# Up-projections of a ConvFFN: the weights' sums and the mixing products on VectorE in place of GpSimd, with VectorE's steps of a tile in a new order

## The chip, the cores and the metric

One core of a Trainium2 chip runs the whole network in one launch. The metric is the time of one execution on the device in microseconds (us). Engines are named as in the profile: PE (TensorE, matmuls), PEld (its weight loads), DVE (VectorE), ACT (ScalarE), POOL (GpSimd), SP (SyncE, which issues all the DMAs spoken of here).

## The reference, cut to what matters

Two layers over 1024 latent tokens and 256 context tokens of width 1024. Each layer ends with a ConvFFN, and the change touches only its up-projection:

```python
D_FF = 2816
def conv_ffn(h, w_up, conv_w, conv_b, w_down):
    a = h @ w_up                                   # 1024 x 5632
    g, u = a[..., :D_FF], a[..., D_FF:]
    gp = jnp.pad(g, ((0, 0), (1, 1), (0, 0)))      # along the tokens
    acc = conv_b + gp[:, 0:T]*conv_w[0] + gp[:, 1:T+1]*conv_w[1] + gp[:, 2:T+2]*conv_w[2]
    return (jax.nn.silu(acc) * u) @ w_down
...
# modulation columns of all layers: silu(c) @ w_mod + b_mod
```

In layer 0 latents and context both go through it, in layer 1 the latents alone. All of it is float32.

## The kernel before

The 2816 features are worked off in 22 tiles of 128 features (`f` = 0 to 21); `head` does the first two and sets up, `turn(f)` does one tile, `end` closes. Features lie on partitions, tokens along the row. Tokens come in chunks: 0 and 1 are the two halves of the latents (512 each), 2 is the context (256).

**Seven products in place of eight.** For the latents, gate and up-projection of a tile are one 2x2 block product: rows are gate weights (`a1`, loaded as `raw[f, 0]`) and up weights (`a2`, `raw[f, 1]`), each cut into two halves of 512 input features (`a11`, `a12`, `a21`, `a22`); columns are the two token halves. Sums of the operands save one of the eight products: s1 = a21 + a22, s2 = s1 - a11, s3 = a11 - a21, s4 = a12 - s2 for the weights (`sum`, line 1694; done on POOL for every tile), and t1 to t4 for the tokens, made once in `head`. The seven products are numbered as in `PROD`; in a turn PE does 6, 5, 7 of tile f, then 1 of the next tile n = f + 1, (context, gate weights, of n), 3 of f, 2 of n, (context, up weights, of f), 4 of f. Products 6, 7 and 4 add up in one bank `y`, 5 and 3 in `z`, 1 and 2 in `x`; ACT and DVE read a bank between two of its products, and the next product may start only then.

**Each product is three matmuls for each quarter of its input,** since every operand is a high part (`...h`, rounded by a cast) and a low part (`...l`, the rest): 12 matmuls of 128x512. The high parts of the s are cast by ACT (`high`, L1698), those of a1 by POOL (`ahigh`, L1678) and of a2 by ACT (L1676); all low parts are subtractions on DVE (`low`, L1702; `alow`, L1683).

**After the products,** with g and su rows of a tile: `s1` (L1984, ACT) copies product 1 out of bank x before product 2 adds to it; `u2` (L1988, DVE) reads bank y after product 6 and before 7; `u3` (L1997) and `c22` (L2000) read y and z after 7; `c12` (L2003) reads z after 3; `c21` (L2006) reads y after 4, in the next turn. `c11` (L1994, ACT) copies bank x after product 2. Then the convolution along the tokens: `conv` (L2013, ACT: centre tap), `conv2` (L2017 and L2018, DVE: the two neighbours), `silu` (L2021, ACT), and `mix` (L2024: times u). The mix of chunks 0 and 1 is done on POOL in the next turn, that of the context on DVE. `store` (L2042) sends su to DRAM, for the down-projection.

**Beside it, in layer 0,** `mod` (L321, DVE; L326, POOL, adds 1 to some columns) works off 53 modulation columns of 1024 products each, for one or both of the two condition vectors, up to three columns in a turn. Each needs its weights in `wm`, a tile with one buffer.

**Order.** PE, DVE, ACT and POOL run their instructions in the order in which the code is written. SP's order is not fixed by hand here; a scheduler places the DMAs. `raw` has two buffers, so `raw[n, 0]` can be loaded when s4 of f has been summed, and `raw[n, 1]` when `alow(f, 1)` is done.

Of the kernel before, what the change touches and what calls it, by code (L numbers as in the profile page):

```python
# [44 lines left out]
def backbone(tc, a):  # L45
    nc = tc.nc
    V, S, P, PE, dma = nc.vector, nc.scalar, nc.gpsimd, nc.tensor, nc.sync
# [1020 lines left out]
    po[3].out(2)  # L1068
    po[2].parts(1)
    turn()  # L1070
    evac(1, 1, b1_1)
    w1 = window(1)
# [547 lines left out]
    class Up:  # L1620
# [144 lines left out]
        def head(self, w, b00, n1):  # L1765
# [49 lines left out]
            x = {k: xlp.tile([128, NLAT], F32, name=f"x{k}", tag=f"x{k}") for k in (2, 3)}  # L1815
            self.spare["st"] = [x[2][:, :512], x[2][:, 512:], x[3][:, :512]]
            for n in ("s1", "s2", "s3"):
                self.sum(2, n)
            self.fs[2] = F(self, 2)
            self.product(2, 1)  # L1820
            self.high(2, "s2")
# [21 lines left out]
            for j, p in enumerate(parts[2:]):  # L1843
                p.high(4, xs(j + 4))
                p.low(4)
            self.sum(2, "s4")
            self.high(2, "s4")
            self.low(2, "s4")
            x.update({k: xlp.tile([128, NLAT], F32, name=f"x{k}", tag=f"x{k}") for k in (6, 7)})
# [5 lines left out]
        def turn(self, f):  # L1855

            me, old = self.fs[f], self.fs[f - 1]
            n = f + 1 if f < NF - 1 else None
            ctx = 2 in self.chunks
            self.product(f, 6)  # L1860
            if f > 2:
                old.c21()
            if n:
                self.load(n, 0)
                self.ahigh(n, 0, P)
            else:
                down = self.down = Down(self)
                down.load(0)
                for e in (0, 1):
                    down.act_load(e)  # L1870
            if f > 2:
                old.mix(1)
                old.mix(0)
                old.store()
            self.ahigh(f, 1, S)
            self.product(f, 5)
            if not n:
                down.act_split(0)
            if f > 3:
                me.u2()  # L1880
            else:
                me.s1()
                me.u2()
                me.c11(True)
            if n:
                self.alow(n, 0)
            self.alow(f, 1)
            if n:
                self.load(n, 1)
            else:  # L1890
                down.load(1)
            if f > 2:
                self.mod()
            self.product(f, 7)
            if not n:
                down.act_split(1)
                self.context(f, 1)
            if n:
                for s in ("s1", "s2", "s3"):
                    self.sum(n, s)  # L1900
                new = self.fs[n] = F(self, n)
                self.product(n, 1)
            me.u3()
            me.c22()
            if f == 2:
                old.rest()
            else:
                self.mod()
            if not n:
                down.split(0)  # L1910
            else:
                if n > 3:
                    new.s1()
                new.open()
                self.context(n, 0)
                new.gate(2)
                for s in ("s2", "s1", "s3"):
                    self.high(n, s)
                    self.low(n, s)
            self.product(f, 3)  # L1920
            me.c12()
            for c in (0, 1):
                me.conv(c)
                me.conv2(c)
            self.mod()
            if n:
                self.product(n, 2, "w" if n == 3 else None)
                if n > 3:
                    new.c11()
                self.sum(n, "s4")  # L1930
                self.context(f, 1)
            for c in self.chunks:
                if c == 2:
                    me.conv(2)
                    me.conv2(2)
                me.silu(c)
            if n:
                self.high(n, "s4")
                self.low(n, "s4")
            if ctx:  # L1940
                me.mix(2, V, self.bank[f, "c", 1])
            self.product(f, 4)

        def end(self):

            me = self.fs[NF - 1]
            self.down.split(1)
            me.c21()
            me.mix(0, V)
            me.mix(1)  # L1950
            me.store()

    class F:
# [323 lines left out]
    down = up.down  # L2277
# [19 lines left out]
    for d in range(8):  # L2297
        f = down.product(1, d, (NF - 4, NF - 3))
# [608 lines left out]
    down = up.down  # L2907
# [296 lines left out]
```

## Time and profile before

| | us |
|---|---|
| median of 3 runs | 2892.46 (2890.66 to 2894.56) |
| the profiled execution | 2893.4 |
| its span, first to last instruction | 2891.5 |
| up-projection of layer 0, tiles 2 to 21 (first matmul of tile 2 to first matmul of tile 21) | 765.11 to 1263.86 |
| up-projection of layer 1, the same | 2222.86 to 2605.07 |

The rows quoted further down give the start of an instruction in us from the span's start, its length, engine, source line, operation and tiles, and in brackets the idle time of the engine before it and what ended that. In the chain of waits each row is start, length, engine and line. Groups give the count, the busy time and the mean of one in ns. A busy PE is not a PE at its peak: matmuls overlap, so what a tile costs is read from the start of one tile to the start of the next.

### The profile page before, as it was taken

What the parts mean: (1) busy time and instruction counts of PE and PEld (TensorE: products, weight loads), DVE (VectorE), ACT (ScalarE), POOL (GpSimd) and SP (SyncE); (2) the same over time, 40 slices, a digit from 0 to 9 for tenths busy, and PEclk for the clock granted to TensorE, in tenths of its full rate; (3) what the DMA queues carried; (4) which work ended last, traced back from release to release, by engine and by line L of the source; (5) the groups of instructions that cost most, each with busy time, mean ns of one, the idle gap of its engine ahead of it and who ended that gap; (6) DMA issues with size and microseconds to landing.
All of it is one profiled execution on the core that took longest, in us unless ns stands there. A gap on an engine that the chain in (4) does not pass through costs nothing.

```text
span 2891.5 us, 40129 instructions
## 1 busy us (share of the span) xinstructions
PE 2782.2 (96%) x14654; PEld 2315.7 (80%) x14654; DVE 2246.1 (78%) x3648; ACT 1243.8 (43%) x2518; POOL 1072.6 (37%) x1066
## 2 busy tenths in 40 slices
PE   7988999999999999999999998999999999999997
PEld 3857888887888887888888777999877777777886
DVE  5688888879888887778777887888668666669766
ACT  5525888824433332331002445888634333333104
POOL 2142444762244445421012443444331445552112
PEclk9999999999999999999999999999999999999998
DMA  6144001283143433363221010000141222226311
GB/s 229 70 141 139 15 24 58 85 276 107 49 133 127 134 114 122 130 234 112 68 72 50 30 37 23 1 1 1 39 139 49 80 81 86 75 95 227 94 59 59
DMA packets 97229, 264.89 MB, mean 92 GB/s; under 512 B 11908, under 2 KB 21060, under 8 KB 96904
## 3 DMA queue, kind: packets, MB, share of 16 engines
q1 hardware_dynamic: 97032, 262.33, 27.1%
q8 instruction: 115, 1.88, 0.3%
q14 instruction: 82, 0.67, 0.1%
HBM read 212.53 MB, written 49.75 MB: 91 GB/s over the span
## 4 chain that ended last, share of the span: by engine, by line
PE 46%; DVE 16%; DMA 4%; issue 4%; POOL 3%; ACT 3%; DVEq 0%; POOLq 0%; SPq 0%; ACTq 0%
PE d L72 18%; PE y L72 4%; PE p L72 4%; PE b L72 4%; PE pv L1277 3%; DMA raw<-in_wup 3%; PE x L72 3%; PE z L72 2%; POOL x L1694 2%; PE T L1264 2%; DVE x L2017 2%; DVE x L2018 2%; DVE a2l L1683 1%; PE S L1197 1%; PE qk L72 1%
## 5 line engine op out<-in xcount | busy, mean ns | idle before, releaser
L2100 DVE SCALAR_TENSOR_TENSOR x<-d,mod,x 128x512 f32<-128x512 f32 (+1 forms) x352 | 255.0, 735 | 95.6 <-PE d L72 93.4
L1246 POOL TENSOR_SCALAR p<-p,sm 128x1280 f32<-128x1280 f32 x128 | 171.3, 1338 | 288.3 <-DVE sm L1245 199.7
L1267 DVE TENSOR_TENSOR tl<-T,th 128x512 fp32r<-128x512 f32 x328 | 225.5, 687 | 46.7 <-ACT th L1266 41.3
L1277 PE MATMUL pv<-th,v 128*128 128x256 f32 x976 | 254.1, 309 | 1.4 <-ACT vo L1406 1.0
L1220 DVE TENSOR_REDUCE mx<-S 128x1 f32<-128x512 f32 (+1 forms) x400 | 233.9, 585 | 11.0 <-PE S L1199 3.8
L72 PE MATMUL d<-act,wh 128*128 128x512 f32 (+1 forms) x832 | 232.0, 365 | 0.0
L1266 ACT CAST th<-T 128x512 fp32r<-128x512 f32 x328 | 192.2, 586 | 84.4 <-PE T L1264 76.5
L2083 ACT CAST act<-act 128x512 fp32r<-128x512 f32 (+1 forms) x110 | 61.5, 577 | 383.8 <-PE d L72 215.5
L1694 POOL TENSOR_TENSOR x<-raw 128x512 f32<-128x512 f32 x80 | 119.4, 1492 | 271.8 <-DMA raw<-in_wup 191.7
L72 PE MATMUL b<-h,wh 128*128 128x512 f32 (+1 forms) x752 | 207.8, 364 | 6.0 <-DVE h L489 4.1
L1264 PE MATMUL T<-ident,p 128*128 128x128 f32 x1280 | 193.0, 272 | 1.5 <-POOL p L1246 1.5
L72 PE MATMUL x<-h,a1h 128*128 128x512 f32 x608 | 190.9, 395 | 0.0
L1264 PEld LDWEIGHTS T<-ident,p 128*128 128x128 f32 x1280 | 156.5, 140 | 34.9 <-POOL p L1246 3.2
L1277 PE MATMUL pv<-tl,v 128*128 128x256 f32 x656 | 177.4, 282 | 0.0
L1277 PEld LDWEIGHTS pv<-th,v 128*128 128x128 f32 x976 | 173.4, 189 | 2.4 <-ACT vo L1406 1.5
L72 PEld LDWEIGHTS d<-act,wh 128*128 128x128 f32 x832 | 149.8, 189 | 27.2
L72 PEld LDWEIGHTS b<-h,wh 128*128 128x128 f32 x752 | 133.6, 190 | 36.4 <-DVE h L489 5.5
L2024 POOL TENSOR_TENSOR su<-x,su 128x512 f32<-128x512 f32 x78 | 131.3, 1696 | 55.4 <-DVE su L2006 44.3
L72 PE MATMUL d<-act,wl 128*128 128x512 f32 (+1 forms) x416 | 151.8, 365 | 0.0
L1984 ACT COPY su<-x 128x512 f32<-128x512 f32 x40 | 23.4, 586 | 289.6 <-PE x L72 209.1
L1237 ACT ACTIVATE p<-S,mx,rq 128x512 f32<-128x512 f32 (+1 forms) x192 | 136.2, 712 | 12.4 <-DVE mx L1228 10.8
L72 PE MATMUL b<-h,wl 128*128 128x512 f32 (+1 forms) x376 | 136.3, 363 | 2.5 <-DVE wl L111 2.4
(520 smaller groups left out, 8205.0 us busy)
## 6 DMA issues: line engine op xcount, KB each, us to landing
raw<-in_wup SPq DMA_DIRECT2D x86, 512.0 KB, 3.4
wm<-in_wmod SPq DMA_DIRECT2D x72, 512.0 KB, 3.6
act<-d_act SPq DMA_DIRECT2D x88, 256.0 KB, 4.0
raw<-in_wdn SPq DMA_DIRECT2D x44, 512.0 KB, 4.4
raw<-in_wout SPq DMA_DIRECT2D x32, 512.0 KB, 3.3
d_act<-su SPq DMA_DIRECT2D x22, 640.0 KB, 3.0
d_act<-su SPq DMA_DIRECT2D x22, 512.0 KB, 2.9
raw<-in_win SPq DMA_DIRECT2D x20, 512.0 KB, 3.6
```

The source lines that it names most:

```text
L72: PE.matmul(out, w, x, start=first and i == 0, stop=last and i == n - 1, skip_group_check=more)
L1220: V.reduce_max(mx[:, j : j + 1], s, axis=AX.X)
L1237: S.activation(o, s, AF.Exp, scale=self.scale, bias=self.mx[:, 3:4], accum_out=self.sm[:, j : j + 1])
L1246: P.tensor_scalar(out=self.p, in0=self.p, scalar1=sm[:, 3:4], scalar2=1.0, op0=ALU.mult, op1=ALU.mult)
L1264: PE.transpose(tb[:, (2 * j + i) * 128 : (2 * j + i) * 128 + 128], rows[i].p[:, c : c + 128], ident)
L1266: S.copy(hi, tb)
L1267: V.tensor_sub(lo, tb, f32(hi))
L1277: PE.matmul(out[0], st, mv, start=(u + j == 0 and x == 0), stop=(u + j == n - 1 and x == len(ops) - 1))
L1694: eng.tensor_tensor(out=t, in0=self.src(f, x), in1=self.src(f, y), op=op)
L2024: eng.tensor_mul(self.s_of(c), self.t[c], self.s_of(c) if u is None else u)
L2083: S.copy(hi, f32(lo))
L2100: V.scalar_tensor_tensor(out=x, in0=b, scalar=mod[self.l, c // 2][:, 40 + d : 41 + d], in1=x, op0=ALU.mult, op1=ALU.add)
```

## The change

All four sums of a tile and the mix of chunks 0 and 1 go from POOL to DVE. In a turn the sums s1 to s3 come after `c22`, and right behind them the casts and low parts of s2, s1, s3; the copy `s1` of product 1 comes after those casts. `conv(0)` is issued ahead of `c12`, `silu` right behind each `conv2`; s4's sum, cast and low part come ahead of the context's convolution, then the mix of chunk 1; the mix of chunk 0 comes in the next turn behind `c21`. In layer 0 the second `mod` of a turn stands behind the low parts and the third at the turn's end; turn 2 now has two where it had one. The arithmetic is the same.

```diff
@@ head
             for n in ("s1", "s2", "s3"):
-                self.sum(2, n)
+                self.sum(2, n, V)
...
-            self.sum(2, "s4")
+            self.sum(2, "s4", V)
@@ turn
             self.product(f, 6)
             if f > 2:
                 old.c21()
+                old.mix(0, V)
+                old.store()
             if n:
                 self.load(n, 0)
                 self.ahigh(n, 0, P)
...
-            if f > 2:
-                old.mix(1)
-                old.mix(0)
-                old.store()
...
             if n:
-                for s in ("s1", "s2", "s3"):
-                    self.sum(n, s)
                 new = self.fs[n] = F(self, n)
                 self.product(n, 1)
             me.u3()
             me.c22()
             if f == 2:
                 old.rest()
-            else:
-                self.mod()
-            if not n:
-                down.split(0)
-            else:
+            if n:
+                for s in ("s1", "s2", "s3"):
+                    self.sum(n, s, V)
+                for s in ("s2", "s1", "s3"):
+                    self.high(n, s)
+                    self.low(n, s)
                 if n > 3:
                     new.s1()
                 new.open()
                 self.context(n, 0)
                 new.gate(2)
-                for s in ("s2", "s1", "s3"):
-                    self.high(n, s)
-                    self.low(n, s)
+            else:
+                down.split(0)
+            self.mod()
             self.product(f, 3)
+            me.conv(0)
             me.c12()
+            me.conv(1)
             for c in (0, 1):
-                me.conv(c)
                 me.conv2(c)
-            self.mod()
+                me.silu(c)
             if n:
                 self.product(n, 2, "w" if n == 3 else None)
                 if n > 3:
                     new.c11()
-                self.sum(n, "s4")
-                self.context(f, 1)
-            for c in self.chunks:
-                if c == 2:
-                    me.conv(2)
-                    me.conv2(2)
-                me.silu(c)
-            if n:
+                self.sum(n, "s4", V)
                 self.high(n, "s4")
                 self.low(n, "s4")
+                self.context(f, 1)
+            me.mix(1, V)
             if ctx:
+                me.conv(2)
+                me.conv2(2)
+                me.silu(2)
                 me.mix(2, V, self.bank[f, "c", 1])
+            self.mod()
             self.product(f, 4)
@@ end
             me.mix(0, V)
-            me.mix(1)
```

Instructions as issued, at three places. The first is DVE in one tile of layer 1, from `alow(f, 1)` on, before (x2_22105 and so on are the spare tiles that hold sums and convolutions):

```order
L1683 TENSOR_TENSOR a2l_22028<-raw_22821,a2h_22027 128x512
L1997 TENSOR_TENSOR su_22838<-y_22921,su_22838 128x512
L2000 TENSOR_TENSOR su_22838<-z_22942,su_22838 128x512
L1702 TENSOR_TENSOR s2l_22996<-x2_22105,s2h_22995 128x512
L1702 TENSOR_TENSOR s1l_23000<-x2_22105,s1h_22999 128x512
L1702 TENSOR_TENSOR s3l_23004<-x3_22106,s3h_23003 128x512
L2003 TENSOR_TENSOR g_22855<-z_22942,x6_22224 128x512
L2017 SCALAR_TENSOR_TENSOR x6_22224<-g_22855,convw_61,x6_22224 128x512
L2018 SCALAR_TENSOR_TENSOR x6_22224<-g_22855,convw_61,x6_22224 128x512
```

The same stretch of DVE with the change (line numbers from 1860 on are up to 4 lower):

```order
L1683 TENSOR_TENSOR a2l_22028<-raw_22821,a2h_22027 128x512
L1993 TENSOR_TENSOR su_22835<-y_22922,su_22835 128x512
L1996 TENSOR_TENSOR su_22835<-z_22942,su_22835 128x512
L1694 TENSOR_TENSOR x2_22105<-raw_22958 128x512
L1694 TENSOR_TENSOR x2_22105<-x2_22105,raw_22938 128x512
L1694 TENSOR_TENSOR x3_22106<-raw_22938,raw_22958 128x512
L1702 TENSOR_TENSOR s2l_22992<-x2_22105,s2h_22991 128x512
L1702 TENSOR_TENSOR s1l_22996<-x2_22105,s1h_22995 128x512
L1702 TENSOR_TENSOR s3l_23000<-x3_22106,s3h_22999 128x512
L1999 TENSOR_TENSOR g_22867<-z_22942,x6_22224 128x512
L2013 SCALAR_TENSOR_TENSOR x6_22224<-g_22867,convw_61,x6_22224 128x512
```

Three sums now stand on DVE between c22 and the low parts. The second place is ACT in a tile of layer 1, before:

```order
L1676 CAST a2h<-raw 128x512
L1984 COPY su<-x 128x512
L1698 CAST s2h<-x_22106 128x512
L1698 CAST s1h<-x_22105 128x512
L1698 CAST s3h<-x_22105 128x512
L2013 ACTIVATE x_22225<-g,convw 128x512
```

and ACT with the change:

```order
L1676 CAST a2h<-raw 128x512
L1698 CAST s2h<-x_22106 128x512
L1698 CAST s1h<-x_22105 128x512
L1698 CAST s3h<-x_22105 128x512
L1980 COPY su<-x 128x512
L2009 ACTIVATE x_22225<-g,convw 128x512
```

The copy that frees bank x for product 2 moved behind the three casts. The third place is SP in a tile of layer 0 (raw: up-projection weights, wm: modulation weights, d_act: the store), before:

```order
L307 DMA wm_9316<-in_wmod 128x1024
L2042 DMA d_act0_7024<-su_9027 128x1280
L1644 DMA raw_9417<-in_wup 128x1024
L307 DMA wm_9421<-in_wmod 128x1024
L307 DMA wm_9455<-in_wmod 128x1024
L1644 DMA raw_9600<-in_wup 128x1024
```

and SP with the change:

```order
L307 DMA wm_9371<-in_wmod 128x1024
L2038 DMA d_act0_7024<-su_9027 128x1280
L1644 DMA raw_9421<-in_wup 128x1024
L307 DMA wm_9424<-in_wmod 128x1024
L307 DMA wm_9503<-in_wmod 128x1024
L1644 DMA raw_9606<-in_wup 128x1024
```

Nothing moved in SP's order: although the code now asks for the store ahead of the load of the next gate weights, that load (the last row) is still placed ahead of the next store.

## Rows read from the trace of the kernel before

**Rows 1.** The page: the span, and busy time (share of the span) and instructions of each engine.

```profile
span 2891.5 us, 40129 instructions
PE 2782.2 (96%) x14654; PEld 2315.7 (80%) x14654; DVE 2246.1 (78%) x3648; ACT 1243.8 (43%) x2518; POOL 1072.6 (37%) x1066
```

**Rows 2.** Timeline of PE: the first matmul of product 6, which opens a tile; tiles 3, 4, 5, 6 and 21 of layer 0, then tiles 2, 4, 9, 10 and 21 of layer 1.

```profile
790.37 0.39 PE L72 MATMUL y<-h,s2h 128*128 128x512 f32 x1
820.00 0.63 PE L72 MATMUL y<-h,s2h 128*128 128x512 f32 x2
845.25 0.39 PE L72 MATMUL y<-h,s2h 128*128 128x512 f32 x1
870.50 0.39 PE L72 MATMUL y<-h,s2h 128*128 128x512 f32 x1
...
1263.86 0.63 PE L72 MATMUL y<-h,s2h 128*128 128x512 f32 x2
...
2222.86 0.40 PE L72 MATMUL y<-h,s2h 128*128 128x512 f32 x1
2264.97 0.62 PE L72 MATMUL y<-h,s2h 128*128 128x512 f32 x2
2366.01 0.39 PE L72 MATMUL y<-h,s2h 128*128 128x512 f32 x1
2385.46 0.39 PE L72 MATMUL y<-h,s2h 128*128 128x512 f32 x1
2605.07 0.39 PE L72 MATMUL y<-h,s2h 128*128 128x512 f32 x1
```

**Rows 3.** Timeline of PE: the first matmul of product 7, with the idle time before it, in tile 3 of layer 0 and in tile 21 of layer 1.

```profile
798.93 1.22 PE L72 MATMUL y<-h,s3h 128*128 128x512 f32 x2 [2.84 <-DVE x L1988]
...
2614.34 1.19 PE L72 MATMUL y<-h,s3h 128*128 128x512 f32 x2 [3.56 <-DVE x L1988]
```

**Rows 4.** The chain of waits in layer 1, tiles 10 and 11 (start, length, what): once round, from one end of a2l to the next.

```profile
2392.45 1.72 DVE a2l L1683
2394.19 3.92 DMA raw<-in_wup
2398.24 1.30 POOL x L1694
...
2400.92 0.63 ACT s2h L1698
...
2408.49 0.61 ACT s4h L1698
...
2410.56 0.60 DVE x L1988
2411.15 1.13 DVE a1l L1683
2412.29 1.71 DVE a2l L1683
```

**Rows 5.** The chain of waits in layer 0, tiles 13 and 14.

```profile
1077.38 0.44 POOL mod L326
1077.82 1.27 POOL x L1694
1079.10 4.50 DMA raw<-in_wup
...
1107.69 4.07 DMA raw<-in_wup
```

**Rows 6.** Groups of DVE's and POOL's instructions in layer 1, tiles 4 to 20 (us 2264 to 2605; count | busy us, mean ns of one | idle before), and one line of who waited for whom in the same stretch (us in total, times, longest).

```profile
L2017 DVE SCALAR_TENSOR_TENSOR x<-g,convw,x 128x512 f32<-128x512 f32 x35 | 33.9, 970 | 0.0
L1683 DVE TENSOR_TENSOR a2l<-raw,a2h 128x512 fp32r<-128x512 f32 x17 | 25.8, 1519 | 0.0
L1702 DVE TENSOR_TENSOR s2l<-x,s2h 128x512 fp32r<-128x512 f32 x17 | 19.0, 1118 | 96.3 <-ACT s2h L1698 96.3
L1702 DVE TENSOR_TENSOR s1l<-x,s1h 128x512 fp32r<-128x512 f32 x17 | 11.5, 679 | 0.0
...
L1678 POOL TENSOR_SCALAR a1h<-raw 128x1024 fp32r<-128x1024 f32 x17 | 18.7, 1102 | 62.2 <-DMA raw<-in_wup 55.2 <-PE y L72 7.0
...
DVE s4l L1702 <- ACT s4h L1698: 22.1, 17, 1.3
```

**Rows 7.** Layer 0: one form of the modulation columns on DVE over the whole up-projection (ns, shortest/median/longest; first and last start), then a group of DVE's in tiles 5 to 17 (us 845 to 1188).

```profile
L321 DVE CUSTOM_DVE_ANT_0 wm<-wm,silc,bmod x53: 1271/1285/2410, 791.7 to 1244.7; 128x1024 f32<-128x1024 f32 x53
...
L1683 DVE TENSOR_TENSOR a1l<-raw,a1h 128x1024 fp32r<-128x1024 f32 x13 | 27.0, 2074 | 9.7 <-POOL a1h L1678 9.7
```

**Rows 8.** Stretches: their length, busy time (count) of PE, PEld, DVE, ACT and POOL, then PE's granted clock as a share of full speed, the DMA share and GB/s; layer 0, tile 3 and tiles 8 to 12; layer 1, tiles 4 to 20.

```profile
790.00:820.00 30.00, 27.16 (x136) 22.73 (x134) 25.49 (x34) 9.88 (x17) 14.08 (x13) 0.94 0.37 116
921.00:1050.00 129.00, 127.56 (x663) 107.47 (x662) 109.50 (x138) 41.82 (x70) 58.16 (x61) 1.00 0.37 124
2264.00:2605.00 341.00, 334.10 (x1433) 268.21 (x1432) 215.49 (x256) 113.25 (x188) 174.42 (x154) 1.00 0.24 82
```

**Rows 9.** Layer 1, tile 2, where POOL summed s4 early: timeline rows of SP (the load of `raw[3, 0]`), POOL (its cast) and DVE (the step ahead of product 7).

```profile
2218.81 0.33 SPq L1644 DMA_DIRECT2D raw<-in_wup  x1
...
2222.88 1.05 POOL L1678 TENSOR_SCALAR a1h<-raw 128x1024 fp32r<-128x1024 f32 x1 [4.10 <-PE w L72]
...
2229.33 0.68 DVE L1988 TENSOR_TENSOR x<-y,su 128x512 f32<-128x512 f32 x1
```

## The prediction

> **What bounds the kernel now.** I began with the page: PE is busy 96% of the span, DVE 78% [rows 1]. A busy PE says little here, so I read the start of each tile on PE's timeline next [rows 2]. It shows the floor of a tile, the period where nothing stalls: 870.50 - 845.25 = 25.25 us in layer 0, 2385.46 - 2366.01 = 19.45 in layer 1 (seven products of 2.78; the two for the context add 5.8). Whatever lies above that is what the change can win:
>
> - layer 0, tile 3: 820.00 - 790.37 = 29.63, so 4.4 over;
> - layer 0, tiles 4 to 20: 443.86 - 17 x 25.25 = 14.6 over;
> - layer 1, tiles 2 and 3: 42.11 - 2 x 19.45 = 3.2 over;
> - layer 1, tiles 4 to 20: 340.10 - 17 x 19.45 = 9.45 over;
> - layer 1, tile 21: 3.56 of waiting [rows 3] and some 1.5 of slow clock, 5.1. (Tile 3 of layer 0 gives the 1.5: 2.84 of its 4.4 is waiting; the granted clock of the stretch is 0.94 [rows 8], and the first pair of matmuls behind the wait took 1.22 where a pair takes 0.63 [rows 2, 3], so it ran at the lower of PE's two levels.)
>
> Together 36.8 us, 1.3%. No more can come from these tiles.
>
> Where PE waits, it is product 7 that waits for `u2` [rows 3], that is, DVE comes late. Why, the chain shows. In layer 1 it is a ring that never touches PE [rows 4]: a2l ends at 2394.17, the load of the next up weights goes out, lands, POOL makes s1 and s2 (1.30 each), ACT casts, DVE makes the low parts, c12, four conv2 steps, waits for s4's cast, then s4l, c21, u2, a1l, a2l, which ends at 2414.00. Once round is 19.83, more than the floor of 19.45; where a landing is slower it is longer. In layer 0 the ring runs over POOL: in tiles 13 to 15 POOL's sum of s4, which lets the next load go, stands behind a modulation column's increment, which waits for DVE, and load follows load at 1079.10 and 1107.69, 28.6 apart [rows 5].
>
> **What DVE gains and pays.** It takes six more instructions a tile: four sums and two mixes of 128x512. A low part of that size takes 0.68, and the next one starts after 0.60 [rows 4, 6], so 6 x 0.60 = 3.6. It gets back what POOL's steps cost it: in layer 1 a2l takes 1.52 though it is half as long as an a1l of 1.13, so 0.6 would do; s2l 1.12 in place of 0.68; the L2017 steps 0.97 in place of 0.75 [rows 4, 6]. That is 0.9 + 0.45 + 2 x 0.22, and a1l at 1.70 in the mean of those tiles adds some 0.5: 2.3 a tile. In layer 0 a1l takes 2.07 [rows 7], and modulation passes run from 1.27 to 2.41. Net, DVE's load grows by about 1.3 in layer 1, where it is busy 63% of the time, and hardly in layer 0, where it is 85% [rows 8]. POOL keeps a1h, the increments and some memsets; a1h can still hold DVE by up to its own 1.10 [rows 6].
>
> The Trainium skill (SBUF — State Buffer, Who interferes with whom) says that VectorE and GpSimd share a pair of ports under an exclusive lock, so that the second to come blocks until the first is done. The doubled durations agree; by that rule a sum costs DVE nearly as much on POOL as on DVE, and DVE's load would not grow at all, which would leave the sum below as it is.
>
> **Layer 1, the new ring.** Load 4.05 (2394.19 to 2398.24), three sums 1.8, cast 0.1 beyond them, three low parts 1.8, c12 0.6, four conv2 at 0.75 or less, 2.9, then the wait for s4's cast: it was 1.3 [rows 6] and grows by the c11 copy that ACT now does ahead of it, to 1.9 (s4's sum lies in it); s4l, mix 1, c21, mix 0, u2 3.0; a1l 1.13, a2l 0.6. Sum 17.9; with a1h's whole 1.1 against it 19.0. Below 19.45, so PE sets the pace: u2 can end 3.6 after a tile's start and has until 5.56. All of the 9.45 goes. **Tile 21** waits since c21 started only 5.6 after the tile's start, with two splits of the down-projection's inputs ahead of u2; c21 now starts at 1.3, u2 ends near 4.4, and the 5.1 go too. **What is next late** is ACT: the copy of product 1 stands behind the three casts now. Counted from a tile's start, a2l ends at 5.35, the weights land at 9.4, c22 ends at 9.8, s2 at 11.0, the casts at 12.7, the copy at 13.2; product 2 wants bank x at 13.9. It fits by 0.6.
>
> **Layer 0, the new ring.** Load 4.1 to 4.5 [rows 5], sums and cast 1.9, low parts 1.8, one modulation column, c12 and conv2 3.5, s4 and the wait for its cast 1.9, s4l and mix 1 1.2, the context's conv2, silu and mix 2.0, another column, c21, mix 0 and u2 1.8, a1l and a2l 2.3. Columns come as pairs and singles in turn, so these two make three passes of 1.28 or 3.9. Sum 24.5 with 4.2 for the load. The floor is 25.25; a1h's 1.1 could make it 25.6, 0 to 6 us over 17 tiles. I take 1.5. The increments no longer hold any load, since no sum stands behind them on POOL. 13.1 of 14.6 goes.
>
> **The starts.** Tile 2 carries f = 1's whole convolution on DVE besides its own, so u2 of tile 3 is late. Contention goes (two or three us), two sums' worth and a second modulation column come in; I find u2 of tile 3 at the same place within 0.6 and leave the 4.4. In layer 1 the start gets worse: POOL made s4 early, so the load of raw[3, 0] went out at 2218.81; now s4's sum comes behind the token parts at about 2228.5, the load lands near 2232, a1h ends near 2233 and a1l near 2234.3, 0.6 after product 1 wants it; u2 of tile 2 moves from 2229.33 [rows 9] to about 2229.8, since DVE waits for s4's cast. I take 1.1 more loss.
>
> **Stores and loads.** The code asks for the store ahead of the next gate weights, and behind a store that waits for mix 0 they would land too late. SP's order as built doesn't do that: load, store, load as before. Nothing.
>
> **The sum.** 2893.4 - 13.1 - 9.45 - 5.1 + 1.1 = 2866.9 for the profiled execution, which lay 0.9 above the median: 2866. Between its own bounds (0 to 6 in layer 0, 0 to 3 in the starts) 2860 to 2873.
>
> **Rivals.**
>
> - *DVE's ring binds layer 0.* For it: 24.5 is a sum of steps without hand-overs, 85% busy is much for an engine that waits in order. Against: contention falls. At 26.0 a tile the loss is 17 x 0.75 = 12.8 in place of 1.5: 2877.
> - *ACT's copy binds layer 1.* It has 0.6 to spare; if weights land 1.1 later (a store or another load beside them), each of 17 tiles loses 0.5: 2875.
> - *The ring stays.* If the landing of the weights and the hand-overs, not POOL's speed, make the ring, the tiles keep their periods, and only tile 21 gains: 2888 to 2893, no change.
> - *Slower: DVE is oversubscribed in layer 0.* If increments and a1h still hold it by their full length and each modulation pass keeps a part of its 2.41, the ring is 27.2: 17 x 1.95 = 33 in place of 14.6, and waits as long as tile 3's bring the slow clock's 1.5 in every second tile, 12 more. With layer 1's 13.5 won: 2893.4 + 18.4 + 12 - 13.5 = 2910. It decides from a ring of 26.9, where the loss eats all gains.
>
> The Trainium skill (Perfetto Trace Analysis, Optimizing Scalar/DVE Operations) advises to move work off VectorE where it is saturated, even to GpSimd, though for those two it doubts the use. At 85% busy its first half speaks against this change and for the last rival; 2.41 against 1.27 for one modulation pass [rows 7] speaks for the second half.
>
> **How the numbers follow.** Chances: forecast 0.58, DVE's ring in layer 0 0.18, ACT's copy 0.08, the ring stays 0.07, slower 0.09. The measurement can tell about 0.2%, 6 us, from no change; the first three are faster by more, so 0.84 faster, 0.07 the same, 0.09 slower. The range leaves out the last two and a little below: down to 2856, where the starts lose nothing and all 36.8 goes, and up to 2885, past both partial cases with the longest ring I'd grant them (26.5 a tile).
>
> **What will show it.** Right: layer 1's tiles at 19.45 from tile 4 on, layer 0's at 25.3 or so, no wait for u2 but in the first tiles, a2l near 0.7 and modulation passes near 1.28, chain on PE. Wrong: periods of 26 in layer 0 with DVE busy nine tenths; product 2 waiting for the copy (L1980) in layer 1; a chain that still goes round over the loads; a load sitting behind a store.

## The result and the profile after

The median is 2870.99 us (2870.58 to 2874.77, 5 runs) against 2893.5 (2890.66 to 2897.86, 5 runs of the kernel before beside them): a ratio of 0.9924, 95% interval 0.9909 to 0.9938. So 22.5 us were won where 26.5 were forecast. The profiled execution has a span of 2869.2 us.

The page after, where [rows 1] stood before: the span, busy time and instructions.

```profile
span 2869.2 us, 40136 instructions
PE 2775.6 (97%) x14654; PEld 2318.1 (81%) x14654; DVE 2272.8 (79%) x3886; ACT 1241.0 (43%) x2518; POOL 700.2 (24%) x828
```

DVE has 238 instructions more and POOL as many fewer. POOL lost 372 us of busy time, DVE took up only 27: the steps that moved are shorter on DVE, and others of DVE's became shorter with them gone from POOL. What it brought is on PE's timeline, in the starts of tiles 3, 4 and 21 of layer 0 and 2, 3, 4, 5 and 21 of layer 1 (before: [rows 2]).

```profile
790.83 0.39 PE L72 MATMUL y<-h,s2h 128*128 128x512 f32 x1
821.08 0.39 PE L72 MATMUL y<-h,s2h 128*128 128x512 f32 x1
1250.35 0.39 PE L72 MATMUL y<-h,s2h 128*128 128x512 f32 x1
2213.67 0.40 PE L72 MATMUL y<-h,s2h 128*128 128x512 f32 x1
2234.26 0.39 PE L72 MATMUL y<-h,s2h 128*128 128x512 f32 x1
2257.49 0.39 PE L72 MATMUL y<-h,s2h 128*128 128x512 f32 x1
2276.95 0.62 PE L72 MATMUL y<-h,s2h 128*128 128x512 f32 x2
2588.20 0.39 PE L72 MATMUL y<-h,s2h 128*128 128x512 f32 x1
```

Tiles 4 to 20 take 1250.35 - 821.08 = 429.27 in layer 0, 17 times 25.25, and 2588.20 - 2257.49 = 330.71 in layer 1, 17 times 19.45. Nothing is lost there any more. What is left lies in the starts: tile 3 of layer 0 takes 30.25, tiles 2 and 3 of layer 1 take 20.59 and 23.23.

DVE's groups in layer 1, tiles 4 to 20 (before: [rows 6]), then in layer 0's whole up-projection (before: [rows 7], where a1l is that of tiles 5 to 17; in those tiles it takes 1.21 now).

```profile
L1683 DVE TENSOR_TENSOR a2l<-raw,a2h 128x512 fp32r<-128x512 f32 x17 | 11.6, 685 | 0.0
L1702 DVE TENSOR_TENSOR s2l<-x,s2h 128x512 fp32r<-128x512 f32 x17 | 11.8, 692 | 2.8 <-ACT s2h L1698 2.8
L1993 DVE TENSOR_TENSOR su<-y,su 128x512 f32<-128x512 f32 x17 | 11.8, 692 | 52.6 <-PE y L72 52.6
...
L321 DVE CUSTOM_DVE_ANT_0 wm<-wm,silc,bmod 128x1024 f32<-128x1024 f32 x53 | 68.6, 1295 | 0.8
L1683 DVE TENSOR_TENSOR a1l<-raw,a1h 128x1024 fp32r<-128x1024 f32 x20 | 24.3, 1215 | 0.9 <-POOL a1h L1678 0.9
```

a2l fell from 1.52 to 0.69, s2l from 1.12 to 0.69, a1l of layer 0 from 2.07 to 1.22. The wait that was left at u2 (L1984) in those 17 tiles of layer 1, in total, times and longest:

```profile
DVE x L1984 <- PE y L72: 6.3, 17, 0.4
```

DVE now waits for PE: it is early.

**Where 4.3 us went.** From the start of tile 21 of layer 0 to that of tile 2 of layer 1 it was 2222.86 - 1263.86 = 959.00 before [rows 2], and is 2213.67 - 1250.35 = 963.32. The change doesn't touch this stretch. PE's order there differs by one matmul in layer 0's down-projection (a stage whose order a scheduler sets, unlike the up-projection's), and PE's timeline shows one wait that grew, at the start of layer 1's attention, where a product named `T` follows three score matmuls. The row of before, then that of after:

```profile
1770.63 0.39 PE L72 MATMUL T<-wh,h 128*128 128x256 f32 x1 [2.28 <-DVE v L2470]
```

```profile
1757.01 0.58 PE L72 MATMUL T<-wh,h 128*128 128x256 f32 x1 [6.01 <-DVE v L2466]
```

In the built programs the PSUM banks differ from that stage on: two of its tiles swap banks 4 and 6, and the swap is handed on, since a tile takes a bank that came free. The first `T` takes bank 4 in both programs. Before, the last tile in bank 4 had long been read; after, it holds the product `v` of token tile 5 (v5 below), and its evacuation stands on DVE behind three steps for the norm of a query. So the first `T` waits 6.0, where before only the second one waited 2.3. The 24 matmuls behind the wait are slow in both, 5.35 after and 4.63 before (last section), so that wait and matmuls together are 4.45 longer, about the 4.3.

The other kernels agree. In the four whose first `T` waits 6.0 (after, e1, e8, e11) the stretch takes 962.8 to 966.2; in the seven where a `T` waits 2.3 it takes 957.2 to 961.6. So the wait is certain, but stretches with the same wait differ by as much as the 4.3.

### The profile page after: what moved, and what is told of

Read it like the earlier page. It is cut to its first block, busy times and chain, and to the rows that moved or that the text cites. A ratio compares the mean times of both kernels' runs of the same rounds, so it can differ in the third digit from the quotient of the medians.

```text
span 2869.2 us, 40136 instructions
## 1 busy us (share of the span) xinstructions
PE 2775.6 (97%) x14654; PEld 2318.1 (81%) x14654; DVE 2272.8 (79%) x3886; ACT 1241.0 (43%) x2518; POOL 700.2 (24%) x828
## 4 chain that ended last, share of the span: by engine, by line
PE 64%; DVE 7%; ACT 2%; issue 1%; POOL 1%; DMA 0%; DVEq 0%; SPq 0%; ACTq 0%; POOLq 0%
PE d L72 18%; PE y L72 11%; PE z L72 7%; PE x L72 7%; PE p L72 6%; PE pv L1277 3%; PE b L72 3%; PE T L1264 2%; PE qk L72 1%; PE S L1197 1%; PE S L1199 1%; PE S L1198 1%; PE v L72 1%; DVE x L2014 0%; DVE mx L1220 0%
## 5 line engine op out<-in xcount | busy, mean ns | idle before, releaser
L1678 POOL TENSOR_SCALAR a1h<-raw 128x1024 fp32r<-128x1024 f32 x38 | 43.2, 1138 | 675.4 <-DMA raw<-in_wup 457.7
L1698 ACT CAST s2h<-x 128x512 fp32r<-128x512 f32 x40 | 24.9, 622 | 392.5 <-PE x L72 254.9
L1237 ACT ACTIVATE p<-S,mx,rq 128x512 f32<-128x512 f32 (+1 forms) x192 | 136.2, 712 | 12.7 <-DVE mx L1228 11.2
L72 PEld LDWEIGHTS x<-h,a1h 128*128 128x128 f32 x608 | 114.8, 189 | 26.6
```

The source lines that it names most:

```text
L72: PE.matmul(out, w, x, start=first and i == 0, stop=last and i == n - 1, skip_group_check=more)
L1237: S.activation(o, s, AF.Exp, scale=self.scale, bias=self.mx[:, 3:4], accum_out=self.sm[:, j : j + 1])
L1678: P.tensor_scalar(out=hi[:, c], in0=self.raw[f, s][:, c], scalar1=1.0, scalar2=0.0, op0=ALU.mult, op1=ALU.add)
```

## The experiments

The losses are read as in the prediction: periods above 25.25 or 19.45, summed over the tiles named, in us, of the profiled execution. Each ratio is to runs of the kernel before on the same chip. "Between" runs from tile 21 of layer 0 to tile 2 of layer 1. Medians are of 4 or 5 runs, but 3 for before, 10 for e2 and 2 for e11.

| kernel | median | ratio (95%) | layer 0: 2-3 | 4-20 | between | layer 1: 2-3 | 4-20 |
|---|---|---|---|---|---|---|---|
| before | 2892.46 | | 4.4 | 14.6 | 959.0 | 3.2 | 9.4 |
| after | 2870.99 | 0.9924 (0.9909 to 0.9938) | 5.0 | 0.0 | 963.3 | 4.9 | 0.0 |
| e1 order only | 2934.75 | 1.0143 (1.0128 to 1.0159) | 6.9 | 32.6 | 966.2 | 10.1 | 18.6 |
| e2 engine only | 2899.08 | 1.0019 (1.0010 to 1.0028) | 7.0 | 0.6 | 955.4 | 13.0 | 24.7 |
| e3 sums only | 2872.41 | 0.9926 (0.9912 to 0.9941) | 4.2 | 0.4 | 959.9 | 5.0 | 0.0 |
| e4 mixes only | 2911.32 | 1.0060 (1.0043 to 1.0077) | 7.5 | 31.0 | 957.2 | 7.0 | 7.7 |
| e5 bank | 2866.93 | 0.9909 (0.9896 to 0.9923) | 6.2 | 0.0 | 958.4 | 4.9 | 0.0 |
| e6 early s4, v | 2867.53 | 0.9909 (0.9896 to 0.9923) | 6.4 | 0.0 | 958.9 | 3.6 | 0.0 |
| e7 increments | 2884.25 | 0.9969 (0.9957 to 0.9981) | 5.9 | 3.5 | 961.6 | 3.2 | 7.4 |
| e8 POOL loaded | 2922.14 | 1.0099 (1.0085 to 1.0113) | 9.4 | 18.7 | 962.8 | 10.8 | 21.5 |
| e9 least | 2906.46 | 1.0040 (1.0028 to 1.0053) | 0.9 | 13.3 | 960.3 | 5.2 | 19.5 |
| e10 start and bank | 2860.35 | 0.9886 (0.9870 to 0.9901) | 2.7 | 0.0 | 952.6 | 3.3 | 0.0 |
| e11 e8, copy first | 2924.34 | 1.0106 (1.0087 to 1.0125) | 8.4 | 20.1 | 963.9 | 8.8 | 17.5 |
| e12 least, with mixes | 2865.89 | 0.9906 (0.9889 to 0.9922) | 2.0 | 0.0 | 959.7 | 6.1 | 0.0 |

### Engine or order: e1 to e4

Theory A is the prediction's: POOL's speed, its queue and its contention with DVE make the rings, so the engine decides. Theory B: the order decides.

**e1, order only.**

```diff
-                    self.sum(n, s, V)
+                    self.sum(n, s)
...
-                self.sum(n, "s4", V)
+                self.sum(n, "s4")
...
-                old.mix(0, V)
+                old.mix(0)
...
-            me.mix(1, V)
+            me.mix(1)
```

(and the same for the sums in `head`)

> The changed kernel with all sums and the mixes of chunks 0 and 1 back on POOL, so that only the new order is left. Theory A (POOL's speed and its contention with DVE make the ring, so the engine decides): the ring of layer 1 keeps POOL's sums of 1.3 each, tiles 4 to 20 of layer 1 stay at 19.7 to 20.5 and those of layer 0 at 25.5 to 27, in all 2884 to 2900 us. Theory B (the order decides: columns and convolutions no longer stand ahead of the weights): the tiles run at their floors, 19.45 and 25.25, and the time is that of the changed kernel, 2871.

It is much slower than both kernels, beyond what either theory gave: 2934.75. The part around POOL of its chain of waits in layer 1, which comes round after 20.6, at the last row (`issue` is time for which the chain names no cause; from 2442.91 POOL waits for `c21`, from 2446.63 DVE is still at a1l):

```profile
2441.61 1.30 POOL su L2020
2442.91 1.19 issue
2444.13 1.30 POOL su L2020
2445.43 1.03 POOL a1h L1678
2446.63 1.00 issue
2447.63 0.69 DVE a2l L1683
2448.34 3.28 DMA raw<-in_wup
2451.76 1.31 POOL x L1694
2453.13 1.30 POOL x L1694
...
2462.21 1.31 POOL su L2020
```

The new order puts the mixes ahead of a1h. In the changed kernel, with the mixes on DVE, that holds up no tile behind the first ones; on POOL both mixes, a1h and two sums stand in one ring. Theory B falls: the order alone is a loss of 1.4%.

**e2, engine only**: the kernel before with `V` given to its sums and to the mixes of chunks 0 and 1.

```diff
-                old.mix(1)
-                old.mix(0)
+                old.mix(1, V)
+                old.mix(0, V)
...
-                    self.sum(n, s)
+                    self.sum(n, s, V)
...
-                self.sum(n, "s4")
+                self.sum(n, "s4", V)
```

> The kernel before with the sums and mixes on DVE at their old places, so that only the engine is changed. Theory A: no sum is left behind an increment on POOL and DVE's steps are as short as in the changed kernel, so the tiles of both layers lie at their floors or up to 0.3 above them, 2868 to 2878 us. Theory B: waits for u2 stay in half of the tiles, 2883 to 2893. In the old order both mixes stand ahead of u2, which costs 0.6 of its slack of some 2 us and nothing in the time.

Layer 0 goes to its floor in tiles 4 to 20, as theory A has it. Layer 1 gets worse than before, and the whole is slower by 0.1 to 0.3%, outside what either theory gave. The reason stands on DVE's timeline in a tile of layer 1 (a2l, then the three sums, u3, c22) and on PE's (the first matmul of product 3):

```profile
2434.21 0.68 DVE L1683 TENSOR_TENSOR a2l<-raw,a2h 128x512 fp32r<-128x512 f32 x1
2438.09 0.69 DVE L1694 TENSOR_TENSOR x<-raw 128x512 f32<-128x512 f32 x1 [3.20 <-DMA raw<-in_wup]
...
2440.03 0.68 DVE L1997 TENSOR_TENSOR su<-y,su 128x512 f32<-128x512 f32 x1
2440.75 0.69 DVE L2000 TENSOR_TENSOR su<-z,su 128x512 f32<-128x512 f32 x1
```

```profile
2441.59 0.70 PE L72 MATMUL z<-h,s4h 128*128 128x512 f32 x2 [0.82 <-DVE su L2000]
```

In the old order the sums stand ahead of u3 and c22. On POOL that held up none of DVE's steps; on DVE the queue stops for the weights' landing, c22 comes late, and product 3 waits for bank z (14 times in tiles 4 to 19, 15.7 in all). So theory A was incomplete: the engine needs the new place of the sums.

**e3, sums only** (e1's diff without its first two changes) and **e4, mixes only** (without its last two):

> The changed kernel with the mixes of chunks 0 and 1 back on POOL: only the sums are on DVE. Theory A, with the sums as its main part: the ring no longer touches POOL except for a1h, two mixes of 1.3 to 1.7 beside DVE cost it about 1 us a tile, which both layers have to spare: tiles at 19.45 and 25.25 to 25.4, 2866 to 2874 us. Rival: contention from any of POOL's 128x512 steps is what counts, and the mixes keep tiles at 19.6 and 25.6 or more, 2876 to 2885.

> The changed kernel with the sums back on POOL: only the mixes are on DVE. Theory A: the sums stay in the ring, tiles 4 to 20 of layer 1 at 19.6 to 20.2, those of layer 0 at 25.4 to 27, 2880 to 2892 us. Rival (contention by the mixes was the loss): floors of 19.45 and 25.25, 2866 to 2874.

e3 has its tiles at both floors: in the new order the move of the mixes brings tiles 4 to 20 nothing. That its time is level too is in part chance. Its banks are those of the kernel before, so `T` waits 2.3 and the stretch between is 3.4 shorter than in the changed kernel; but it takes 1.8 more ahead of tile 2 of layer 0, and 2.9 more from tile 21 of layer 1 to the end, where the down-projection waits 3.4 for a cast (0.7 in the changed kernel). Whether the mixes on POOL cause that was not tried. e4 keeps losses like those of before in layer 1 and twice as large in layer 0, and is slower than its expectation had it. In the new order the sums carry the gain in tiles 4 to 20.

### POOL's queue and its neighbourhood: e7, e8, e11

**e7, increments**, the kernel before with L326 on DVE for layer 1's columns:

```diff
-                P.tensor_scalar(out=mod[l, w][:, i : i + 1], ...
+                (V if l else P).tensor_scalar(out=mod[l, w][:, i : i + 1], ...
```

> The kernel before with one edit: the increments of layer 1's modulation columns (128x1) are done by DVE and not by POOL, so that no sum of POOL's stands behind a wait for DVE's columns. Theory A (that queue makes the long tiles 13 to 17 of layer 0, 11.6 us over the floor): these lose 3 or less, layer 1 is as before, 2881 to 2886 us. Rival (POOL's contention with DVE, or the landing of the column's weights, makes them): they stay 8 or more above the floor, 2889 to 2893.

24 instructions of 128x1 on another engine win 11.1 of the 14.6 us that layer 0 lost in tiles 4 to 20, and 0.3% of the time. With [rows 5] this shows that the sum of s4, which stood behind them in POOL's queue, made most of that loss. The remaining 3.5 I put down to the ring with POOL's slow sums; no run tries that apart.

**e8, POOL loaded**, the changed kernel with six sums in each turn behind a1h that nothing reads:

```diff
+            for _ in range(6):
+                P.tensor_tensor(out=self.dead, in0=self.dead, in1=self.dead, op=ALU.add)
             self.ahigh(f, 1, S)
             self.product(f, 5)
```

> The changed kernel with work added on POOL: in every turn, behind a1h, six sums of 128x512 on a tile of its own that nothing else reads. Theory A (a step on POOL lengthens DVE's steps beside it): DVE's steps in the 8 us behind a1h grow by 0.3 to 1.1 each, some 4 us of DVE a tile; layer 0, where DVE has about 3 us to spare, goes above its floor (25.6 to 28 a tile), layer 1 up to 20; 2875 to 2915 us. Rival (POOL only mattered through what waited for its results): DVE's steps keep 0.69, the tiles stay at 25.25 and 19.45, 2870 to 2872.

Nothing waits for these sums, and yet 51 us are lost against the changed kernel, more than I expected. POOL's rows and DVE's in a tile of layer 1:

```profile
2433.07 7.82 POOL L1876 TENSOR_TENSOR dead<-dead 128x512 f32<-128x512 f32 x6
```

```profile
2433.22 1.97 DVE L1685 TENSOR_TENSOR a1l<-raw,a1h 128x1024 fp32r<-128x1024 f32 x1
2435.11 1.52 DVE L1685 TENSOR_TENSOR a2l<-raw,a2h 128x512 fp32r<-128x512 f32 x1
2438.15 0.69 DVE L1997 TENSOR_TENSOR su<-y,su 128x512 f32<-128x512 f32 x1 [1.52 <-PE y L72]
2438.88 0.69 DVE L2000 TENSOR_TENSOR su<-z,su 128x512 f32<-128x512 f32 x1
2440.02 1.41 DVE L1696 TENSOR_TENSOR x<-raw 128x512 f32<-128x512 f32 x1 [0.46 <-DMA raw<-in_wup]
2441.47 0.69 DVE L1696 TENSOR_TENSOR x<-x,raw 128x512 f32<-128x512 f32 x1
```

a1l, a2l and the first sum take 0.75, 0.83 and 0.72 more than without POOL beside them, 2.3 together, all in the ring. The tile went from 19.45 to 20.53, so by estimate the same ring without POOL's load takes 20.53 - 2.3 = 18.2. It is not the ring that the prediction summed to 17.9, which went from s4's low part over the mixes and u2 to a1l. Here the chain goes from s4's sum over the load of the gate weights and a1h:

```profile
2449.00 3.47 DMA raw<-in_wup
...
2452.64 1.05 POOL a1h L1680
```

u3 and c22, which read one operand from PSUM, keep their 0.69 under the same load. The Trainium skill (SBUF — State Buffer, Who interferes with whom) says just this: a VectorE step with two inputs in SBUF contends with a GpSimd step that reads SBUF; one with at most one input there, outside VectorE's two-port fast modes, does not. The rows agree.

**e11**: e8 with `new.s1()` ahead of the casts.

```diff
+                if n > 3:
+                    new.s1()
                 for s in ("s2", "s1", "s3"):
                     self.high(n, s)
                     self.low(n, s)
-                if n > 3:
-                    new.s1()
```

> The kernel of e8 (six sums added on POOL) with the copy of product 1 ahead of the casts, as in the kernel before. Theory A, by e8's waits (with weights that land late the copy behind the casts holds product 2 by 1.1 to 1.5 a tile): layer 1 falls from 20.53 to 19.5 to 20.0 a tile, layer 0 stays near 26.6; 2905 to 2913 us. Rival (the ring over load and a2l sets 20.53, the copy is only where it shows): 20.4 or more, 2920 to 2924.

I was wrong: tiles stay at 20.5. In e8 product 2 did wait for the copy, in 16 tiles by 1.1 at most, but with the copy out of the way the wait is at u2 (16 tiles, 1.2 at most): the ring over loads and low parts sets the same pace.

### The least change: e9 and e12

**e9**: the kernel before with only a turn's sums moved, behind c22 and onto DVE.

```diff
-                for s in ("s1", "s2", "s3"):
-                    self.sum(n, s)
                 new = self.fs[n] = F(self, n)
                 self.product(n, 1)
             me.u3()
             me.c22()
+            if n:
+                for s in ("s1", "s2", "s3"):
+                    self.sum(n, s, V)
...
-                self.sum(n, "s4")
+                self.sum(n, "s4", V)
```

> The kernel before with one thing changed: the four sums of a turn are on DVE, the three of s1 to s3 right behind c22 (not ahead of u3, where the engine-only kernel had them); head, mixes and all other steps as before. Theory A' (what counts is that no sum is on POOL and that no sum waits for its load ahead of u3 and c22): both layers at their floors, up to 0.3 above in layer 0; with the old head layer 1 starts with a loss of 3.2 or less, tile 21 gains its 5; the PSUM bank is the one of before, so the 4.3 are not lost; 2862 to 2868 us. Rival (columns and mixes must move too): layer 0 at 25.6 or more or layer 1 at 19.6 or more, 2870 to 2885.

This failed by 40 us, and showed why the mixes can matter. Groups of e9 in layer 1: the mixes on POOL, then a1l and a2l.

```profile
L2025 POOL TENSOR_TENSOR su<-x,su 128x512 f32<-128x512 f32 x32 | 56.3, 1781 | 0.0
L1683 DVE TENSOR_TENSOR a1l<-raw,a1h 128x1024 fp32r<-128x1024 f32 x16 | 36.8, 2302 | 30.2 <-POOL a1h L1678 30.2
L1683 DVE TENSOR_TENSOR a2l<-raw,a2h 128x512 fp32r<-128x512 f32 x16 | 28.3, 1771 | 0.0
```

In the old order the two mixes follow a1h on POOL, and a1l and a2l wait for a1h too: the four always run side by side, and a1l and a2l take 2.2 longer together than in the changed kernel, in the ring again. In e3 the mixes stand on POOL ahead of a1h, a1l starts when they are done, and a1l takes 1.23.

**e12**: e9 with `old.mix(1, V)` and `old.mix(0, V)`, nothing else.

> The kernel of e9 (before, with a turn's sums on DVE behind c22) with one more thing changed: the mixes of chunks 0 and 1 are on DVE too, at their old place ahead of u2. So it is the old order, columns and copies included, with two engines changed and the three sums moved. Theory A'' (e9 lost by the two mixes that POOL ran beside a1l and a2l, 2.30 and 1.77 there against 1.2 and 0.7): with POOL quiet behind a1h, layer 1 goes from 20.5 to its floor of 19.45 a tile, layer 0 to 25.25 or up to 0.3 above, tile 21 of layer 1 gains its 5; 2860 to 2868 us. Rival (the old places of columns and of s4's sum make e9's ring, since a1l waits for a1h there): layer 1 at 19.9 or more, 2875 to 2900.

```profile
L1683 DVE TENSOR_TENSOR a1l<-raw,a1h 128x1024 fp32r<-128x1024 f32 x16 | 19.6, 1225 | 4.4 <-POOL a1h L1678 4.1
L1683 DVE TENSOR_TENSOR a2l<-raw,a2h 128x512 fp32r<-128x512 f32 x17 | 11.6, 685 | 0.0
```

The two mixes are worth 40.6 us here and nothing in e3's tiles 4 to 20. Both layers run at their floors with columns, copies and convolutions in the old order. Of the new order only one step is needed: the sums behind c22.

### What is lost beside the tiles: e5, e6, e10

**e5, bank**: the changed kernel with the last tile's mix of chunk 1 back in `end`.

```diff
-            me.mix(1, V)
+            if n:
+                me.mix(1, V)
...
             me.mix(0, V)
+            me.mix(1)
             me.store()
```

> The changed kernel, but the mix of chunk 1 of the last tile goes back to its old place in end, on POOL. In the build this moves one pair of PSUM banks (4 and 6) back to where the kernel before has them from the down-projection of layer 0 on: at the start of layer 1's attention the first product named T then takes a bank that has long been free. Theory A (the 4.3 us lost between layer 0's tile 21 and layer 1's tile 2 are a wait of that T for a bank that v5's evacuation frees late): PE's wait there falls from 6.0 to nothing with 2.3 at the next T, as before, and the time to 2866 to 2868 us. Rival (the 4.3 are scatter of one profile, or come from the down-projection): 2870 to 2872, the wait stays or the time is lost elsewhere.

In the build the edit moves banks 4 and 6 back. PE's row that now stands for the 6.01:

```profile
1759.70 0.39 PE L72 MATMUL T<-wh,h 128*128 128x256 f32 x1 [2.29 <-DVE v L2468]
```

The stretch between the up-projections fell from 963.3 to 958.4, the median by 4.1. The intervals of the two ratios overlap, so it is the wait that carries this, not the medians.

**e6**: the changed kernel with s4's sum early in `head`, and v5's evacuation ahead of the query's steps.

```diff
             self.low(2, "s1")
+            self.sum(2, "s4", V)
...
-            self.sum(2, "s4", V)
             self.high(2, "s4")
...
     keep_value(4)
-    q7_1.rest()
     keep_value(5)
+    q7_1.rest()
```

> The changed kernel with two more edits: in head, the sum of s4 stands on DVE right behind the low part of s1, not behind the token parts; and ahead of layer 1's attention v5's evacuation stands ahead of the last step of q7_1's rope on DVE. Theory A (tile 3 of layer 1 is late since raw[3, 0] is loaded only after s4's sum; the T product waits for v5's evacuation, not for its bank as such): load of raw[3, 0] goes out 8 to 10 us earlier, tiles 2 and 3 of layer 1 lose 1 to 2.5 us in place of 4.9, PE's wait for T falls from 6.0 to about 3; 2863 to 2867 us. Rival (DVE's own load of the start makes tile 3 late): tile 3 stays at 23, 2867 to 2869.

(What stands ahead of v5 there are the three steps for the query's norm, not its rope.) The wait for `T` fell to 3.12, as expected, with the bank still the bad one. Layer 1's start lost 3.6, not 1 to 2.5. The load of raw[3, 0] went out 6.2 ahead of tile 2's start where it had been 4.15 behind it, and a1l no longer waited; but from a1l (2217.20) to u2 of tile 3 (2236.93) DVE was idle for 1.7 us in all, and u2 was late by 1.2 still. The late load was 1.3 of the 4.9. DVE's own load makes part of the rest, as the rival had it; in tile 3 product 2 also waits 1.05 for ACT's copy of product 1 (L1980), which stands behind the three casts.

**e10**: e5 and e6 together, and in turn 2 the first `self.mod()` under `if f > 2`.

> The changed kernel with the edits of e5 and e6 together, and without the first of the two columns of turn 2. Theory A (DVE's own load makes tile 3 of layer 0 late; bank, s4 and v5's order add up): tile 3 of layer 0 loses 3 to 4.5 in place of 5.0 to 6.4, tiles 2 and 3 of layer 1 3.6 as in e6, PE waits 2.3 or less for T; 2861 to 2864 us. Rival (what one edit frees, the next wait takes): 2865 to 2868, as each alone.

2860.35, the best of all, 10.6 below the changed kernel and a little below what was expected. No `T` waits any more. The profile is of its fastest run, 4.7 below the median, so the 952.6 of the stretch between may be too good by as much. Tile 3 of layer 0 lost 2.7 with one column fewer on DVE. That tile lost 5.0 in the changed kernel and 6.2 in e5, with the same steps there, so the size of its gain is uncertain by as much.

## Why the prediction was right, point by point

| term | forecast | measured in the profiles |
|---|---|---|
| layer 0, tile 3 | 0 | -0.6 |
| layer 0, tiles 4 to 20 | +13.1 | +14.6 |
| layer 1, tiles 2 and 3 | -1.1 | -1.7 |
| layer 1, tiles 4 to 20 | +9.45 | +9.4 |
| layer 1, tile 21 and behind | +5.1 | +5.4 |
| ahead of tile 2 of layer 0 | 0 | -0.5 |
| between the up-projections | 0 | -4.3 |
| sum | 26.5 | 22.3 |

- **The floors as the most that can be won** were right: tiles 4 to 20 of both layers lie on them, each within 0.02. The 1.5 that the forecast kept back for layer 0 wasn't lost.
- **The cause**, POOL in the ring by its queue, its speed and its neighbourhood, is shown by e7 (queue), e8, and e9 against e12 (neighbourhood), and e3 (all three, for the sums alone). Its speed can be read, 1.30 for a sum (e1) against 0.69 on DVE (e2), but no run sets it apart from the other two.
- **What DVE gains and pays** held. In layer 1 its load per tile went from 215.49/17 = 12.7 [rows 8] to 243.85/17 = 14.3, 1.7 more where 1.3 was forecast: the shorter steps gave back the 2.3 of the forecast, but the six new ones cost 4.0 in place of 3.6. In layer 0 its share stayed at 85%. The rows of both stretches after:

```profile
921.00:1050.00 129.00, 129.00 (x674) 109.84 (x673) 109.98 (x168) 41.80 (x72) 9.86 (x32) 1.00 0.39 128
2257.00:2588.00 331.00, 331.00 (x1431) 268.78 (x1430) 243.85 (x358) 112.10 (x189) 22.40 (x51) 1.00 0.24 86
```

- The advice that the prediction weighed from the Trainium skill (Perfetto Trace Analysis, Optimizing Scalar/DVE Operations), to take work off a saturated VectorE, pointed the wrong way here; its doubt about GpSimd as the taker was right: six more steps a tile left DVE's share of layer 0 where it was.
- **ACT's copy** had 0.6 to spare by the forecast. It ends 0.35 ahead of product 2: the copy starts at 2387.15 and takes 0.58, product 2 starts at 2388.08. The other tiles of layer 1 from 4 on are the same.

```profile
2387.15 0.58 ACT L1980 COPY su<-x 128x512 f32<-128x512 f32 x1
```

```profile
2388.08 0.64 PE L72 MATMUL x<-h,a1h 128*128 128x512 f32 x2
```

- **Layer 1's start** was under-sized, and by other waits than the forecast's. u2 of tile 2 did not move back by 0.5, it moved up by 0.7, since DVE's token parts became shorter, and product 1 hardly waited for a1l. But the load of `raw[3, 0]` went out at 2217.82, 4.15 after the tile's start where it had been 4.05 ahead of it [rows 2, 9], DVE stood idle 1.52 for a1h, and u2 of tile 3 came late: product 7 waited 1.90 for it (1.14 before), at a granted clock of 0.93 over the tile (1.00 before). Tile 3 then lost 3.8, 1.4 before.

```profile
2222.24 1.23 DVE L1683 TENSOR_TENSOR a1l<-raw,a1h 128x1024 fp32r<-128x1024 f32 x1 [1.52 <-POOL a1h L1678]
```

- **The step that failed** is "The sum": it took all that lies outside the two up-projections as unchanged. The order of one stage decided which banks a later one gets, and about 4.3 of the 26.5 went there (e5). With it the forecast of 2866 would have been met: e5 measured 2866.93. That it fits so well is luck in part: the other misses in the table, from -0.6 to +1.5, cancel.
- **What the prediction didn't price apart**: it costed engine and order as one. Each alone is a loss (e2, e1), and it named neither the place of the sums against u3 and c22 (e2), nor that mixes beside a1l and a2l can make a ring of their own (e9). The number was right since the change does both.
- **What doesn't add up in the prediction.** Its own bounds, 0 to 6 and 0 to 3, give 2863 to 2872, not from 2860. Its last rival turns slower at a ring of 26.9 only without its own 12 of slow clock; with them it is 26.2. And its ring of layer 1 left out the path over the gate weights' load and a1h, the one that binds when POOL is loaded (e8).
- **Still open**: why e1 and e4 lose twice as much in layer 0 as the kernel before, and the 0.5 ahead of tile 2, were not tried.

## What to carry to other kernels

Moving work between two engines that wait in order is two edits: the engine, and the place in the new queue. Ask for each moved step what it waits for and what is queued behind it; a sum that waits for a load belongs behind the evacuations that PE waits for. Ask too what the steps left on the old engine run beside: e9 and e12 differ in the engine of the mixes alone, and by 40.6 us. A stage that isn't touched can still lose: when an edit changes the order in which PSUM banks come free, compare which tile shares a bank with which in the stages behind it.

## What was not expected of the hardware

Steps on POOL made the DVE steps beside them up to 1.1 us longer each: a1l took 2.30 beside the mixes (e9) and 1.22 without, a2l 1.77 and 0.69. Sums that nobody waits for did it too, by up to 0.8 (e8). Steps of 128x512 with an operand in PSUM did not change (e8).

A wait on PE can cost more than its length. After the 6.01 without a matmul the mean granted clock was 0.58, so mostly the lower of the two levels, and the 24 matmuls of `T` took 5.35 us where the next 24 of the same shapes took 2.87, at a granted clock of 1.00 (chain of waits of after, then the stretch's row):

```profile
1757.01 5.35 PE T L72 x24
...
1763.06 2.87 PE T L72 x24
```

```profile
1757.00:1763.00 6.00, 5.99 (x28) 5.86 (x29) 0.75 (x2) 0.37 (x1) 0.00 (x0) 0.58 0.00 0
```

The price is not the same each time. The 24 behind the 2.28 of the kernel before (its chain of waits) took 4.63, those behind the 2.29 of e5 3.13.

```profile
1770.63 4.63 PE T L72 x24
```
